# An encoder trunk in two-part fp32: seven half-width products in place of eight for 16 of the 22 up-projection tiles of each feed-forward block

## The chip, the cores and the metric

One Trainium2 chip, one core. The metric is device time in microseconds (us) of one execution. The kernel before takes 2198.45 us, the median of three runs (2198.32 to 2200.83). Smaller is better.

## The reference

Two layers over 512 tokens of 1024 channels. Each layer is a feed-forward block (FFN), a token mixer, a cross-attention into 256 memory tokens and a second FFN, all with a norm ahead and a sum behind. The change is in the FFNs, of which there are four; one step of it is in the cross-attention.

```python
def swiglu(h, w1, w3, w2):            # w1, w3: 1024 x 2816, w2: 2816 x 1024
    return (jax.nn.silu(h @ w1) * (h @ w3)) @ w2

for l in range(DEPTH):                # 2
    x = x + 0.5 * swiglu(rmsnorm(x, ffn1_norm[l]), ffn1_w1[l], ffn1_w3[l], ffn1_w2[l])
    ...                               # mixer
    x = x + mem_cross_attention(rmsnorm(x, xa_norm[l]), rmsnorm(mem, mem_norm[l]),
                                xa_wq[l], xa_wkv[l], xa_wo[l])
    x = x + 0.5 * swiglu(rmsnorm(x, ffn2_norm[l]), ffn2_w1[l], ffn2_w3[l], ffn2_w2[l])
return rmsnorm(x, final_norm)
```

## The kernel before

**Layout.** x lies in SBUF with its channels on the partitions, as eight tiles of 128 channels x 512 tokens (`xall`, also called xT). Every product is made in fp32 with operands in two parts: `split` (L64 to L76) rounds a tile to the width of the PE on ScalarE (`hi`, L72 or L75) and subtracts it from its source on VectorE (`lo`, L73 or L76); `mm3` (L78 to L82) makes hi·hi, hi·lo and lo·hi, three matmuls. So each weight and each activation costs one ACT and one DVE instruction for its split, and three matmuls for each 128 x 128 block of a weight.

**The stream of weights.** `Weights` (L85 to L140) holds all chunks of 128 x 1024 numbers in the order of their use. `load` fetches a chunk (512 KB) by a DMA on the queue of SyncE (SP), seven chunks ahead of its use (HL + RAW); `cut` splits it two ahead. `next` is called once for each chunk by whoever uses it.

**An FFN** (L375 to L410). The 22 column tiles of w1 and w3 are worked in two parts of 11. For a tile, `col_matmul` makes 8 x 3 matmuls of 512 columns (tokens) with a chunk of w1, then as many with a chunk of w3. The gain of the norm is in the split of x (`Norm.part`), its 1/rms is applied behind the products: DVE multiplies the PSUM tile by `rrow` (L390 and L401), ACT takes the silu (L391), POOL (GpSimd) multiplies the two (L402), and the product `ahl` is split for the down projection. `project` (L337) then adds a part's share of the down projection to x (L356, DVE, eight instructions a part), and behind the last part each finished tile of x goes at once into the next norm: `h` on ACT and DVE, its square on ACT (L309), the sum of the squares on POOL (L314).

**The start of the cross-attention** (from L632). The memory lies in SBUF for the whole program, already scaled by its own 1/rms (`memT`). `xattn` splits it with the layer's gain into `mn` (L75 and L76, sixteen instructions), and its first products are `kT`, of 256 columns, from `mn` and the chunks of xa_wk.

**The end.** `finish` turns x over (transposes on PE, L743) while the last part of the down projection is made with tokens on the partitions.

The order of each engine's instructions is fixed when the program is built; an engine takes its instructions in that order. DMAs are issued in order by the engine whose queue they are on.

Of the kernel before, what the change touches and what calls it, by code (L numbers as in the profile page):

```python
# [14 lines left out]
P = 128  # L15
D = 1024
T = 512
# [10 lines left out]
XSCALE = 256.0 ** -0.5  # L28

# Columns of the table of per-channel vectors: name -> columns per layer.  # L30
# [11 lines left out]
def trunk_kernel(ctx: ExitStack, tc: tile.TileContext, ap: dict, out: bass.AP):  # L42
# [4 lines left out]
    wp = ctx.enter_context(tc.tile_pool(name="wp", bufs=3))  # L47
    hp = ctx.enter_context(tc.tile_pool(name="hp", bufs=16))
    sp = ctx.enter_context(tc.tile_pool(name="sp", bufs=19))
# [11 lines left out]
    def h_tile():  # L61
        return hp.tile([P, 512], F32R, tag="h", name="h")
# [15 lines left out]
    def mm3(o, a, b, start, stop):  # L78
        """o += a.T @ b, both in two parts."""
        pe.matmul(o, a[0], b[0], start=start, stop=False)  # L80
        pe.matmul(o, a[0], b[1], start=False, stop=False)  # L81
        pe.matmul(o, a[1], b[0], start=False, stop=stop)  # L82

    # ------------------------------------------------------------------ the stream of weights
    class Weights:  # L85
        """All weight chunks [128, a, b] with a * b <= 1024 in the order of their use: loaded some
        chunks ahead, split two ahead."""
        RAW, HL = 4, 3

        def __init__(self):  # L90
            self.src, self.raw, self.hl, self.at = [], {}, {}, 0

        def cols(self, w, c):
            """Columns c*128.. of a weight of 1024 rows, which lie as [128, 8, 128]."""
            self.src.append((w[c], NK, P))

        def rows(self, w, k, n, lo, hi):
            """Columns lo..hi of the row blocks k..k+n."""
# [6 lines left out]

        def load(self, i):
            if i < len(self.src) and i not in self.raw:
                src, a, b = self.src[i]
                t = wp.tile([P, 1024], F32, tag="raw", name="raw", bufs=self.RAW)
                tv = t[:, :a * b].rearrange("p (a b) -> p a b", b=b)  # L110
                for c in range(0, a, a if i else a // 2):
                    ce = c + (a if i else a // 2)
                    nc.sync.dma_start(tv[:, c:ce], src[:, c:ce])
                self.raw[i] = t

        def cut(self, i):
            if i < len(self.src) and i not in self.hl:
                self.load(i)
                _, a, b = self.src[i]
                if i == len(self.src) - 1:  # L120
                    hi, lo = s_tile([P, 1024], F32R, "whi"), s_tile([P, 1024], F32R, "wlo")
                else:
                    hi = wp.tile([P, 1024], F32R, tag="whi", name="whi", bufs=self.HL)
                    lo = wp.tile([P, 1024], F32R, tag="wlo", name="wlo", bufs=self.HL)
                n = a * b
                step = n if i else n // 2
                for c in range(0, n, step):
                    split(hi[:, c:c + step], lo[:, c:c + step], self.raw[i][:, c:c + step])
                self.hl[i] = tuple(t[:, :n].rearrange("p (a b) -> p a b", b=b) for t in (hi, lo))

        def next(self):
            i = self.at
            self.at += 1
            for j in range(i, i + self.HL):
                self.cut(j)
            if i + self.HL == len(self.src) - 1:
                self.cut(i + self.HL)
            for j in range(i, i + self.HL + self.RAW):
# [10 lines left out]
    for l in range(L):  # L149
        for w1, w3, w2 in (("ffn1_w1", "ffn1_w3", "ffn1_w2"), ("ffn2_w1", "ffn2_w3", "ffn2_w2")):  # L150
            for half in range(2):
                n = NJ // 2
                for j in range(half * n, (half + 1) * n):
                    wts.cols(ap[w1][l], j)
                    wts.cols(ap[w3][l], j)
                if half and w1 == "ffn2_w1" and l == L - 1:
                    for k in [*range(n)] * 2:
                        wts.rows(ap[w2][l], n + k, 1, 0, D)
                else:
                    wts.project(ap[w2][l][half * n * P:(half + 1) * n * P, :], n)  # L160
# [16 lines left out]
    # ------------------------------------------------------------------ x, channels on partitions  # L177
# [29 lines left out]
    # ------------------------------------------------------------------ lower bounds and memory  # L207
# [3 lines left out]
    def lower_bounds():  # L211
        """Softmax over the layers, summed up to each, less the first."""
# [18 lines left out]
    memT = const.tile([P, NK, M], F32, name="memT")  # L231
# [651 lines left out]
```

## Time and profile before

| | |
|---|---|
| median of the runs | 2198.45 us |
| the profiled execution, first to last instruction (span) | 2195.1 us |
| PE busy | 2171.9 us, 99% |
| DVE busy | 1164.9 us, 53% |
| ACT busy | 721.2 us, 33% |
| POOL busy | 316.4 us, 14% |
| mean granted clock of PE | 0.998 |

The profiled execution is known by its span; the median of the runs is 3.35 us above it. A busy PE is one with matmuls in its pipe: two matmuls that follow one another overlap in the rows, so what a matmul costs is the distance from its start to the next one's, not its duration. "Idle before, releaser" at the end of a row says how long the engine had waited and what ended it.

### The profile page before, as it was taken

What the parts mean: (1) busy time and instruction counts of PE and PEld (TensorE: products, weight loads), DVE (VectorE), ACT (ScalarE), POOL (GpSimd) and SP (SyncE); (2) the same over time, 40 slices, a digit from 0 to 9 for tenths busy, and PEclk for the clock granted to TensorE, in tenths of its full rate; (3) what the DMA queues carried; (4) which work ended last, traced back from release to release, by engine and by line L of the source; (5) the groups of instructions that cost most, each with busy time, mean ns of one, the idle gap of its engine ahead of it and who ended that gap; (6) DMA issues with size and microseconds to landing.
All of it is one profiled execution on the core that took longest, in us unless ns stands there. A gap on an engine that the chain in (4) does not pass through costs nothing.

```text
span 2195.1 us, 25372 instructions
## 1 busy us (share of the span) xinstructions
PE 2171.9 (99%) x10166; PEld 1812.4 (83%) x10166; DVE 1164.9 (53%) x1668; ACT 721.2 (33%) x991; POOL 316.4 (14%) x249
## 2 busy tenths in 40 slices
PE   8999999999999999999999999999999999999998
PEld 6888888788988888888888888887889888888886
DVE  6534544777635544345355345357775455543545
ACT  5322223313434422222332223233144443222234
POOL 3100111302200210011021001023121002100102
PEclk9999999999999999999999999999999999999999
DMA  5323332221432333332333233232214323323334
GB/s 207 96 91 101 96 103 94 87 68 49 132 99 88 95 96 96 96 102 87 100 101 99 88 104 98 96 101 77 68 54 129 97 88 96 96 94 99 98 119 156
DMA packets 75253, 216.40 MB, mean 99 GB/s; under 512 B 6912, under 2 KB 6912, under 8 KB 75008
## 3 DMA queue, kind: packets, MB, share of 16 engines
q1 hardware_dynamic: 74272, 213.16, 30.9%
q8 instruction: 80, 1.31, 0.2%
q10 hardware_dynamic: 864, 1.63, 0.2%
q14 instruction: 37, 0.30, 0.0%
HBM read 212.66 MB, written 2.10 MB: 98 GB/s over the span
## 4 chain that ended last, share of the span: by engine, by line
PE 97%; DVE 2%; POOL 1%; ACT 0%; issue 0%; DMA 0%; SPq 0%; POOLq 0%; DVEq 0%; ACTq 0%
PE ps L80 23%; PE ps L81 23%; PE ps L82 23%; PE acc L81 7%; PE acc L80 7%; PE acc L82 7%; PE ps L495 2%; PE ps L617 0%; DVE wlo L73 0%; POOL qk L448 0%; PE ps L618 0%; PE ps L601 0%; PE ps L522 0%; PE ps L259 0%; PE acc L259 0%
## 5 line engine op out<-in xcount | busy, mean ns | idle before, releaser
L73 DVE TENSOR_TENSOR wlo<-raw,whi 128x1024 fp32r<-128x1024 f32 (+1 forms) x403 | 584.2, 1450 | 423.6 <-ACT whi L72 423.6
L72 ACT CAST whi<-raw 128x1024 fp32r<-128x1024 f32 (+1 forms) x403 | 416.8, 1035 | 1183.8 <-PE ps L81 609.9
L80 PE MATMUL ps<-h,whi 128*128 128x512 f32 x1848 | 720.7, 391 | 7.7 <-ACT h L75 7.7
L81 PE MATMUL ps<-h,whi 128*128 128x512 f32 x1848 | 720.9, 390 | 0.6 <-DVE h L76 0.6
L82 PE MATMUL ps<-h,wlo 128*128 128x512 f32 x1848 | 720.3, 390 | 0.0
L80 PEld LDWEIGHTS ps<-h,whi 128*128 128x128 f32 x1848 | 348.1, 188 | 80.7 <-ACT h L75 8.1
L81 PEld LDWEIGHTS ps<-h,whi 128*128 128x128 f32 x1848 | 347.9, 188 | 73.5 <-DVE h L76 1.8
L82 PEld LDWEIGHTS ps<-h,wlo 128*128 128x128 f32 x1848 | 347.8, 188 | 72.5 <-DVE wlo L73 0.2
L402 POOL TENSOR_TENSOR t<-t,t 128x512 f32<-128x512 f32 x88 | 122.2, 1389 | 1022.9 <-ACT whi L72 915.2
L401 DVE TENSOR_TENSOR t<-ps,rrow 128x512 f32<-128x512 f32 x87 | 60.1, 691 | 261.9 <-PE ps L82 261.9
L390 DVE TENSOR_TENSOR t<-ps,rrow 128x512 f32<-128x512 f32 x88 | 60.8, 691 | 127.6 <-PE ps L82 120.9
L80 PE MATMUL ps<-ahl,whi 128*128 128x512 f32 x308 | 119.8, 389 | 0.0
L81 PE MATMUL ps<-ahl,whi 128*128 128x512 f32 x308 | 119.8, 389 | 0.0
L80 PE MATMUL acc<-ahl,whi 128*128 128x512 f32 x308 | 119.8, 389 | 0.0
L81 PE MATMUL acc<-ahl,whi 128*128 128x512 f32 x308 | 119.8, 389 | 0.0
L82 PE MATMUL acc<-ahl,wlo 128*128 128x512 f32 x308 | 119.8, 389 | 0.0
L82 PE MATMUL ps<-ahl,wlo 128*128 128x512 f32 x308 | 118.7, 389 | 0.0
L314 POOL TENSOR_TENSOR sqa<-sqa,sq 128x512 f32<-128x512 f32 x48 | 76.2, 1587 | 140.7 <-ACT sq L309 138.7
L72 ACT CAST ahl<-t 128x512 fp32r<-128x512 f32 x88 | 54.9, 624 | 117.2 <-POOL t L402 117.2
L76 DVE SCALAR_TENSOR_TENSOR h<-xall,vec,h 128x512 fp32r<-128x512 f32 x64 | 73.5, 1171 | 24.3 <-ACT h L75 24.0
L81 PE MATMUL acc<-h,whi 128*128 128x512 f32 x200 | 78.1, 390 | 0.0
L82 PE MATMUL acc<-h,wlo 128*128 128x512 f32 x200 | 78.0, 390 | 0.0
(205 smaller groups left out, 2311.9 us busy)
## 6 DMA issues: line engine op xcount, KB each, us to landing
raw<-in_ffn_w_dram SPq DMA_DIRECT2D x267, 512.0 KB, 3.6
raw<-in_w_in_dram SPq DMA_DIRECT2D x32, 512.0 KB, 3.5
raw<-in_w_out_dram SPq DMA_DIRECT2D x16, 512.0 KB, 3.6
raw<-in_xa_wk_dram SPq DMA_DIRECT2D x16, 512.0 KB, 3.5
raw<-in_xa_wq_dram SPq DMA_DIRECT2D x16, 512.0 KB, 3.5
raw<-in_xa_wv_dram SPq DMA_DIRECT2D x16, 512.0 KB, 3.6
raw<-in_xa_wo_dram SPq DMA_DIRECT2D x16, 512.0 KB, 3.7
raw<-in_ffn_w_dram SPq DMA_DIRECT2D x16, 256.0 KB, 2.6
```

Of the source, the lines that this page charges most:

```text
L72: act.copy(hi, src)
L73: dve.tensor_tensor(lo, src, hi.bitcast(F32), op=ALU.subtract)
L76: dve.scalar_tensor_tensor(lo, src, scale, hi.bitcast(F32), op0=ALU.mult, op1=ALU.subtract)
L80: pe.matmul(o, a[0], b[0], start=start, stop=False)
L81: pe.matmul(o, a[0], b[1], start=False, stop=False)
L82: pe.matmul(o, a[1], b[0], start=False, stop=stop)
L314: pool.tensor_tensor(a, self.sq, s, op=ALU.add)
L390: dve.tensor_tensor(t1, p1, norm.r, op=ALU.mult)
L401: dve.tensor_tensor(t3, p3, norm.r, op=ALU.mult)
L402: pool.tensor_tensor(t3, t1, t3, op=ALU.mult)
L495: pe.matmul(o, kg[g][:, hh, sl], rhs, start=True, stop=True)
```

## The change

**Pairs of tiles.** In each FFN the first 6 of the 22 tiles stay as they were (PLAIN). The other 16 are worked as 8 pairs, and each pair once with w1 and once with w3: 16 blocks in an FFN, 64 in the program. A block is the product of two column tiles of a weight (2 x 128 columns, 1024 rows, seen as 2 x 2 blocks) with the activations (1024 rows in two halves, 512 tokens in two halves of 256). It is made from 7 half products instead of 8 (Strassen's scheme in Winograd's form): 7 x 4 x 3 = 84 matmuls of 256 columns where two `col_matmul` made 48 of 512.

**The right operands** (`Pairs.operands`, L472 to L533): x times gain times 1/rms by DVE (8 instructions of 512), four sums of its quarters by DVE (L493 and L496, 2 instructions of 512 each), and seven splits of 1024 columns (b11, b21, b22, t1 to t4). They are made between the products of tiles 2 to 5 of the same FFN. 1/rms is now in the operands, so the products need no scaling behind them.

**The left operands** (`Weights.load`, `cut`). For a block the SP queue brings two halves of 256 KB (L130, L131) into a tile `wsum`, the first tile (L132, 512 KB) and the lower half of the second (L133, 256 KB). Then a DMA on the queue of GpSimd *adds* the whole second tile (512 KB) to what lies in `wsum` (L134): this makes two of the four sums of left blocks in SBUF. It waits for both halves. DVE makes the other two sums (L163, L164; 512 columns each). Split are r1, s1, s2 (1024 columns each) and w22 (512).

**Behind the products** of a block: three copies of 256 PSUM columns by ACT (`keep`, L537), four sums of a PSUM tile and a kept one in halves of 256 columns by DVE (L592, L610 and, with the product by the gate in the same instruction, L618), the silu on ACT. The gate product is made by DVE (L612, L614, L618); POOL has none in a block. The last two of the seven products of a block are made among the first of the next one (`open`).

**Other steps.** The down projection runs in three parts (8, 8 and 6 tiles) instead of two of 11, so x is added to three times in an FFN. One pool of 38 slots of 4 KB takes the place of three pools. `memT` is no longer kept: each layer loads it again (four DMAs on the SP queue), and DVE multiplies it by its 1/rms (L914, four instructions of 512) right ahead of the splits into `mn`.

```diff
+PLAIN = 6
+PARTS = ((0, 8), (8, 16), (16, 22))
 ...
         def load(self, i):
+            if len(self.src[i]) == 2:
+                c1, c2 = self.src[i]
+                s1, t1 = s_tile([P, NK, P], F32, "wsum"), s_tile([P, NK, P], F32, "raw")
+                t2 = s_tile([P, 4, P], F32, "raw")
+                nc.sync.dma_start(s1[:, :4], c1[:, :4])
+                nc.sync.dma_start(s1[:, 4:], c2[:, :4])
+                nc.sync.dma_start(t1, c1)
+                nc.sync.dma_start(t2, c2[:, 4:])
+                nc.gpsimd.dma_start(s1, c2, accum_op=ALU.add)
...
         def cut(self, i):
+                split(h0, l0, r1)
+                split(h1, l1, s1)
+                dve.tensor_tensor(s2[:, :512], s1[:, 512:], a11, op=ALU.add)
+                dve.tensor_tensor(s2[:, 512:], s2[:, :512], a12, op=ALU.add)
+                split(h2, l2, s2)
+                split(t[:, 0], t[:, 1], a22)
...
+        def block(self, out):
+            w = wts.next()
+            last, self.open = self.open, None
+            z, y, x = ps_tile(), acc_tile(), acc_tile()
+            self.product(z, "a11", "b11", True)
+            c1 = self.keep(z)
+            if last:
+                last[0]()
+            self.product(y, "s1", "t1", True)
+            p5 = self.keep(y)
+            self.product(x, "a12", "b21", True)
+            out.add(0, 0, x, c1)
+            if last:
+                last[1]()
+            self.product(z, "q", "t2", False)
+            u = self.keep(z)
+            self.product(y, "f", "b22", False)
+            out.add(0, 1, y, u)
...
     def xattn(l, norm, after):
         for k2 in range(NK // 2):
+            mt = s_tile([P, 2, M], F32, "mt")
+            nc.sync.dma_start(mt, ap["memT"][:, 2 * k2:2 * k2 + 2])
+            dve.tensor_tensor(mt, mt, memr.rearrange("p (o m) -> p o m", o=1).broadcast_to([P, 2, M]), op=ALU.mult)
             t = s_tile([P, 2, 2, M], F32R, "mn")
             for e in range(2):
                 k = 2 * k2 + e
-                split(t[:, 0, e], t[:, 1, e], memT[:, k], scale=vcol("mem_norm", l, k))
+                split(t[:, 0, e], t[:, 1, e], mt[:, e], scale=vcol("mem_norm", l, k))
```

**Three places of the order.** The first is VectorE in the first FFN. Before, around two tiles (`t1`, `t3` are the scaled PSUM tiles):

```order
L390 TENSOR_TENSOR t_782<-ps,rrow 128x512
L73 TENSOR_TENSOR wlo<-raw,whi 128x1024
L401 TENSOR_TENSOR t_816<-ps,rrow 128x512
L73 TENSOR_TENSOR wlo<-raw,whi 128x1024
L73 TENSOR_TENSOR ahl<-t_816,ahl 128x512
```

In the changed program, one gate block and the first half of the up block behind it, in the steady part (`wsum`: sums of left blocks; `raw`: tiles as loaded):

```order
L77 TENSOR_TENSOR wlo_1779<-raw_1494,whi_1778 128x1024
L592 TENSOR_TENSOR gate_1751<-acc_1763,keep_1776 128x256
L77 TENSOR_TENSOR wlo_1811<-wsum_1493,whi_1810 128x1024
L163 TENSOR_TENSOR wsum_1827<-wsum_1493,raw_1494 128x512
L618 SCALAR_TENSOR_TENSOR up_1621<-ps_1630,gate_1492 128x256
L164 TENSOR_TENSOR wsum_1827<-wsum_1827,raw_1494 128x512
L77 TENSOR_TENSOR ahl_1490<-up_1621,ahl_1490 128x512
L592 TENSOR_TENSOR gate_1751<-acc_1762,keep_1857 128x256
L77 TENSOR_TENSOR wlo_1860<-wsum_1827,whi_1859 128x1024
L77 TENSOR_TENSOR w22_1877<-raw_1495,w22_1877 128x512
L77 TENSOR_TENSOR wlo_1902<-raw_1623,whi_1901 128x1024
L592 TENSOR_TENSOR gate_1752<-ps_1761,keep_1808 128x256
```

For a pair of tiles VectorE had 10 instructions (twice the five above); it now has 23, from `wlo_1779` to the L612 of the next up block: 6 wlo, 2 w22, 4 sums of weights, 2 ahl, 6 sums of 256 columns, L612 and L618 of 256 columns, and L614 of 512.

The second place is VectorE at the start of the first layer's cross-attention. Before (the last additions to x are the two L356):

```order
L76 SCALAR_TENSOR_TENSOR mn<-memT,vec,mn 128x256 x8
L73 TENSOR_TENSOR wlo<-raw,whi 128x1024
...
L356 SCALAR_TENSOR_TENSOR xall<-acc,xall 128x512 x2
L76 SCALAR_TENSOR_TENSOR h<-xall,vec,h 128x512
L356 SCALAR_TENSOR_TENSOR xall<-acc,xall 128x512 x2
L76 SCALAR_TENSOR_TENSOR h<-xall,vec,h 128x512
L73 TENSOR_TENSOR wlo<-raw,whi 128x1024
L76 SCALAR_TENSOR_TENSOR h<-xall,vec,h 128x512 x2
L73 TENSOR_TENSOR wlo<-raw,whi 128x1024
L73 TENSOR_TENSOR kT<-ps,kT 128x256
```

In the changed program:

```order
L430 SCALAR_TENSOR_TENSOR xall<-acc,xall 128x512
L80 SCALAR_TENSOR_TENSOR h<-xall,vec,h 128x512 x2
L914 TENSOR_TENSOR mt<-mt,memr 128x512
L80 SCALAR_TENSOR_TENSOR mn<-mt,vec,mn 128x256 x2
L335 TENSOR_SCALAR v<-acc 128x4
L914 TENSOR_TENSOR mt<-mt,memr 128x512
L938 TENSOR_SCALAR sr<-rcol 128x4
L80 SCALAR_TENSOR_TENSOR mn<-mt,vec,mn 128x256 x2
L914 TENSOR_TENSOR mt<-mt,memr 128x512
L80 SCALAR_TENSOR_TENSOR mn<-mt,vec,mn 128x256 x2
L914 TENSOR_TENSOR mt<-mt,memr 128x512
L80 SCALAR_TENSOR_TENSOR mn<-mt,vec,mn 128x256 x2
```

The splits of the memory, which stood ahead of the last additions to x, now stand behind the last `h`, each pair of them behind its own L914.

The third place is TensorE at the same point of the changed program (before, the first `ps<-mn` follows the last `acc<-h` directly):

```order
L86 MATMUL acc_5046<-h_4976,wlo_5090 128x512
L333 MATMUL acc_5458<-ones_88,sqa_5223 128x1 x4
L84 MATMUL ps_5257<-mn_5228,whi_5133 128x256
L84 MATMUL ps_5291<-mn_5228,whi_5163 128x256
L85 MATMUL ps_5257<-mn_5228,whi_5133 128x256
L86 MATMUL ps_5257<-mn_5228,wlo_5134 128x256
L84 MATMUL ps_5257<-mn_5228,whi_5133 128x256
```

The products that lead to 1/rms of the next norm (L333, from the sum of squares `sqa`, which POOL makes) have moved ahead of the first products with `mn`; before they came behind six of the eight tiles of `kT`. The first two tiles of `kT` (`ps_5257`, `ps_5291`) are now worked side by side, one pair of `mn` after the other.

## Rows read from the trace of the kernel before

**Rows 1.** The page: the span, the busy time of the engines, and the chain that ended last, by engine.

```profile
span 2195.1 us, 25372 instructions
PE 2171.9 (99%) x10166; PEld 1812.4 (83%) x10166; DVE 1164.9 (53%) x1668; ACT 721.2 (33%) x991; POOL 316.4 (14%) x249
PE 97%; DVE 2%; POOL 1%; ACT 0%; issue 0%; DMA 0%; SPq 0%; POOLq 0%; DVEq 0%; ACTq 0%
```

**Rows 2.** The two largest of the three waits of TensorE in the whole span: us in total, times, longest.

```profile
PE ps L80 <- ACT h L75: 7.7, 1, 7.7
PE ps L455 <- DVE atd L482: 6.6, 2, 3.3
```

**Rows 3.** The timeline of TensorE (start and duration in us) in a stretch of products of 512 columns: the first and the last of 49 rows without idle time between them, 48 distances.

```profile
410.18 0.39 PE L80 MATMUL ps<-h,whi 128*128 128x512 f32 x1
...
421.06 0.39 PE L80 MATMUL ps<-h,whi 128*128 128x512 f32 x1
```

**Rows 4.** The timeline of TensorE at the start of the first layer's cross-attention: the last product of 512 columns, the first of 256, and the one 48 distances behind that.

```profile
577.22 0.39 PE L82 MATMUL acc<-h,wlo 128*128 128x512 f32 x1
577.44 0.28 PE L80 MATMUL ps<-mn,whi 128*128 128x256 f32 x1
...
583.20 0.28 PE L80 MATMUL ps<-mn,whi 128*128 128x256 f32 x1
```

**Rows 5.** Groups of instructions on VectorE by form over the whole span: count, then busy us and mean ns of one, then the idle time before them and its releasers.

```profile
L73 DVE TENSOR_TENSOR wlo<-raw,whi 128x1024 fp32r<-128x1024 f32 x387 | 573.1, 1482 | 370.6 <-ACT whi L72 370.6
L73 DVE TENSOR_TENSOR ahl<-t,ahl 128x512 fp32r<-128x512 f32 x88 | 61.2, 697 | 13.1 <-ACT ahl L72 12.8
L390 DVE TENSOR_TENSOR t<-ps,rrow 128x512 f32<-128x512 f32 x88 | 60.8, 691 | 127.6 <-PE ps L82 120.9 <-ACT rrow L326 6.7
L73 DVE TENSOR_TENSOR kT<-ps,kT 128x256 fp32r<-128x256 f32 x16 | 6.7, 416 | 0.0
L76 DVE SCALAR_TENSOR_TENSOR mn<-memT,vec,mn 128x256 fp32r<-128x256 f32 x16 | 6.5, 484 | 0.0
```

**Rows 6.** The timeline of VectorE around two of its splits of weights in the second part of the first FFN.

```profile
303.76 2.33 DVE L73 TENSOR_TENSOR wlo<-raw,whi 128x1024 fp32r<-128x1024 f32 x1 [0.21 <-ACT whi L72]
...
309.20 1.23 DVE L73 TENSOR_TENSOR wlo<-raw,whi 128x1024 fp32r<-128x1024 f32 x1 [0.21 <-ACT whi L72]
```

**Rows 7.** The timeline of POOL in the same stretch: the only instruction there.

```profile
303.72 1.29 POOL L402 TENSOR_TENSOR t<-t,t 128x512 f32<-128x512 f32 x1 [8.46 <-ACT whi L72]
```

**Rows 8.** Groups on ScalarE by form, columns as in rows 5.

```profile
L72 ACT CAST whi<-raw 128x1024 fp32r<-128x1024 f32 x387 | 406.9, 1052 | 1121.0 <-PE ps L81 579.2 <-issue 281.7 <-PE acc L81 155.7
L391 ACT ACTIVATE t<-t 128x512 f32<-128x512 f32 x88 | 55.1, 626 | 1.0 <-DVE t L390 1.0
L72 ACT CAST kT<-ps 128x256 fp32r<-128x256 f32 x16 | 5.9, 366 | 0.0
L75 ACT ACTIVATE mn<-memT,vec 128x256 fp32r<-128x256 f32 x16 | 6.6, 496 | 0.0
```

**Rows 9.** The page's DMA parts: a queue (packets, MB, share of the span of 16 engines), and issues (count, KB each, median us from issue to landing).

```profile
q1 hardware_dynamic: 74272, 213.16, 30.9%
raw<-in_ffn_w_dram SPq DMA_DIRECT2D x267, 512.0 KB, 3.6
raw<-in_ffn_w_dram SPq DMA_DIRECT2D x16, 256.0 KB, 2.6
```

**Rows 10.** The timeline of VectorE from the splits of the memory to the first products of the first layer's cross-attention.

```profile
545.33 3.26 DVE L76 SCALAR_TENSOR_TENSOR mn<-memT,vec,mn 128x256 fp32r<-128x256 f32 x8
...
577.64 0.69 DVE L356 SCALAR_TENSOR_TENSOR xall<-acc,xall 128x512 f32<-128x512 f32 x1 [0.61 <-PE acc L82]
578.25 1.28 DVE L76 SCALAR_TENSOR_TENSOR h<-xall,vec,h 128x512 fp32r<-128x512 f32 x1
579.45 1.21 DVE L73 TENSOR_TENSOR wlo<-raw,whi 128x1024 fp32r<-128x1024 f32 x1
580.59 3.49 DVE L76 SCALAR_TENSOR_TENSOR h<-xall,vec,h 128x512 fp32r<-128x512 f32 x2
```

**Rows 11.** The timeline of POOL in the same stretch: the last two sums of squares of the norm.

```profile
579.80 3.73 POOL L314 TENSOR_TENSOR sqa<-sqa,sq 128x512 f32<-128x512 f32 x2 [0.81 <-ACT sq L309]
```

**Rows 12.** The timeline of TensorE in the first part of the program: two matmuls of 512 columns that follow one another, and the first two at a closer distance.

```profile
12.28 0.63 PE L81 MATMUL ps<-h,whi 128*128 128x512 f32 x1
12.70 0.63 PE L82 MATMUL ps<-h,wlo 128*128 128x512 f32 x1
...
16.11 0.44 PE L80 MATMUL ps<-h,whi 128*128 128x512 f32 x1
16.39 0.39 PE L81 MATMUL ps<-h,whi 128*128 128x512 f32 x1
```

**Rows 13.** The timeline of TensorE behind one of its two waits in the mixer (the time in brackets is the idle time before the row).

```profile
434.13 0.71 PE L455 MATMUL ps<-qkp,ones_r 128*128 128x512 f32 x2 [3.28 <-DVE atd L482]
...
434.98 0.39 PE L81 MATMUL ps<-h,whi 128*128 128x512 f32 x1
435.20 0.39 PE L82 MATMUL ps<-h,wlo 128*128 128x512 f32 x1
```

**Rows 14.** The timeline of TensorE in `finish`: twelve turned blocks, that is three half rows of tokens.

```profile
2123.30 1.47 PE L743 MATMUL ps<-fixed,xall 128*128 128x128 f32 x12
```

**Rows 15.** The timeline of ScalarE there: the copies of those three.

```profile
2126.21 1.55 ACT L744 COPY y<-ps 128x512 f32<-128x512 f32 x3
```

More of the change, by code (lines that the diff above doesn't have):

```diff
@@ L104, in project @@
                     self.rows(w, g[0], len(g), half * 512, (half + 1) * 512)
-        def load(self, i):
[L107 to L114, printed above, removed]
@@ L116, in cut, with ahead @@
-        def cut(self, i):
[L117 to L121, printed above, removed]
-                else:
[L123 to L129, printed above, removed]
+        def ahead(self, i, n):
+            m = 0
+            while i < len(self.src) and m < n:
+                yield i
+                m += 2 if len(self.src[i]) == 2 else 1
+                i += 1
@@ L131, in next, with step, first @@
+        def step(self):
+            while self.todo:
+                if next(self.todo[0], self) is self:
+                    self.todo.pop(0)
+                else:
+                    return
+        def first(self):
+            self.todo.append(self.cut(0))
+            self.step()
         def next(self):
@@ L133, in next @@
             self.at += 1
[L134 to L138, printed above, removed]
+            while self.todo:
+                self.step()
+            block = len(self.src[i]) == 2
+            ahead = [*self.ahead(i, self.SPLIT + block)]
+            if i + self.SPLIT == len(self.src) - 1:
+                ahead.append(i + self.SPLIT)
+            for j in ahead:
+                if j not in self.hl:
+                    self.todo.append(self.cut(j))
+                    if not block or j == i:
+                        while self.todo:
+                            self.step()
+            for j in self.ahead(i, self.LOAD):
                 self.load(j)
@@ L249, in prepare_mem @@
         pr = col_to_row(dg, 2)
-        for k2 in range(NK // 2):
-            t = memT[:, 2 * k2:2 * k2 + 2]
-            dve.tensor_tensor(t, t, pr[:, :M].rearrange("p (o m) -> p o m", o=1).broadcast_to([P, 2, M]), op=ALU.mult)
+        act.copy(memr, pr[:, :M])
     def col_rsqrt(sq, inv, tag, tile=acc_tile):
@@ new lines, in trunk_kernel, with __init__, add, done @@
+    class Gate:
+        def __init__(self):
+            self.t = [tp.tile([P, T], F32, tag="gate", name="gate", bufs=4) for _ in range(2)]
+        def add(self, i, half, ps, t):
+            o = self.t[i][:, half * HT:(half + 1) * HT]
+            dve.tensor_tensor(o, ps[:, :HT], t, op=ALU.add)
+            if half:
+                o = self.t[0] if i == 0 else o
+                act.activation(o, o, AF.Silu, scale=-1.0 if i else 1.0)
+        def done(self, ps):
+            act.activation(self.t[1][:, :HT], ps[:, :HT], AF.Silu, scale=-1.0)
@@ L374, in ffn @@
     def ffn(norm, after, start=None, between=None):
-        n = NJ // 2
-        for half in range(2):
+        pairs = None
+        for lo, hi in PARTS:
             a = []
-            for jj in range(n):
-                if start and half == 0 and jj < 2:
-                    if jj == 0:
+            for j in range(lo, hi):
+                if j >= PLAIN:
+                    ahl = s_tile([P, 2, T], F32R, "ahl")
+                    a.append((ahl[:, 0], ahl[:, 1]))
+                    if j % 2:
+                        gate = Gate()
+                        pairs.block(gate)
+                        pairs.block(Up(gate, a[-2:]))
+                        if between:
+                            next(between, None)
+                    continue
+                if start and j < 2:
+                    if j == 0:
@@ L392, in ffn @@
                 norm.then(left)
+                if j == 2:
+                    pairs = Pairs(norm)
+                    operands = pairs.operands()
+                if j > 1:
+                    next(operands, None)
+                    next(operands, None)
                 if p3 is None:
@@ L407, in ffn @@
                     next(between, None)
-            if half and after is None:
+                if j > 1:
+                    next(operands, None)
+                    next(operands, None)
+            for _ in operands:
+                pass
+            pairs.close()
+            if hi == NJ and after is None:
                 return a
-            project(n, a, 0.5, after if half else (lambda d: None))
+            project(hi - lo, a, 0.5, after if hi == NJ else (lambda d: None), tiles=(acc_tile, ps_tile))
     def mix(l, norm, after):
@@ L789, in trunk_kernel @@
     norm = Norm("ffn1_norm", 0, late=3)
-    wts.cut(0)
+    wts.first()
     for d in range(NK):
```

231 lines of the change are left out of this document (192 added, 39 removed).

## The prediction

> **What bounds the kernel now.** I read the page first. TensorE is busy 99% of the span and is 97% of the chain that ended last [rows 1]. Then its waits: one of 7.7 us at the start of the program, two of 3.3 us in the mixer, nothing worth naming in an FFN [rows 2]. So the kernel is bound by the number of matmuls times the distance between them, and every other engine is spare. The change removes work from TensorE and gives work to VectorE. It pays as far as TensorE goes on without waiting.
>
> **What TensorE saves.** 48 matmuls of 512 columns take 421.06 − 410.18 = 10.88 us, 0.2267 each [rows 3]. 48 of 256 columns take 583.20 − 577.44 = 5.76 us, 0.120 each, a little more than half [rows 4]. A block has 84 of the latter, 10.08 us, where two tiles with one weight took 10.88. It saves 0.80 us, and 64 blocks save **51.2 us**. Seven eighths of 10.88 would be 9.52; the other 0.56 goes to the narrower matmul's extra time.
>
> A rule speaks for more. The Trainium skill (TensorE: Matmul & The Clock Gate, Wait — 56ns, not 53.3ns?) gives the distance of warm matmuls as columns over 2.4 GHz plus some 2.5 ns: 0.109 us for 256 columns and 0.216 for 512, by which the saving would be 64 × (10.36 − 9.17) = 76 us, an estimate from that page. The trace has 0.120 and 0.2267 instead; I take the rows.
>
> **What the blocks ask of the others.** VectorE runs 23 instructions for a pair of tiles, in the 20.16 us of two blocks. Priced by form [rows 5]: 2 w22, 4 sums and L614 at 0.69 are 4.8 us; 2 ahl at 0.68 are 1.4; 6 sums of 256 columns from PSUM at 0.42 and two products at 0.48 are 3.5. The 6 wlo I take at 1.23, not at their mean of 1.48. The mean holds those that run beside a product of POOL, 2.33 us against 1.23 [rows 6, 7], and in the blocks POOL makes no product. That is 7.4. The sum is 17.0 of 20.16 us, 84%: full, but under. ScalarE has 6 casts of 1024 at 1.05, seven of 256 and 512 columns, and the silus, some 12.3 us by its forms [rows 8]; no bound. A wait of VectorE for a transfer or for ScalarE delays what stands behind it (the sums that free PSUM tiles, the splits of the next block). The weights are split about one block ahead, so waits of 2 or 3 us are covered. I put nothing for the steady blocks.
>
> **The transfers.** For a block 1.25 MB come by SP's queue, and the DMA that adds brings 0.5 MB more. In all 16 engines 213.16 MB took 30.9% of the span, 678 us, so 512 KB take 1.67 us of all engines [rows 9]; 1.25 MB take 4.2 of the block's 10.08. No row shows a DMA that adds. From below it costs what a plain one does, 3.6 us from issue to landing, behind the two halves' 2.6 [rows 9]. From above I set no bound but the turning point: it becomes the bound of the blocks when it takes over 5.9 us of all engines, 3.5 times a plain one, or 10.08 us by itself, if one must end before the next begins. SP issues a block's halves about two blocks of work ahead of their split (loads run seven chunks ahead, splits four, and a block counts as two; with the slots that come free in time some 20 us), so 2.6 + 10 us would still be in time. I take no cost; cover: those 20 us. On POOL L134 waits for the two halves; behind it stand the last gate products of the plain tiles (1.39 us each before, and their ahl is used only in the down projection, blocks later) and otherwise the next L134, so this wait has nobody behind it who is in a hurry. On SP the halves wait for free slots as the loads did before.
>
> The Trainium skill (DMA: Bandwidth & Descriptors, Anatomy of one DMA) has a fit for plain transfers issued by GpSimd, 2.0 us plus the bytes over 436 GB/s: 3.2 us for 512 KB, an estimate; by that the sum stays as it is.
>
> **The start of the cross-attention**, twice. Before, the splits of the memory were done 29 us ahead of their use [rows 10], and the product with `mn` followed the last one of the mixer without a gap [rows 4]. Now L914 and the splits stand behind the last `h`. From the last product's end (577.44) on: the last addition ends at 578.33; three h of 0.75 (undisturbed) bring it to 580.6, and as they ran (1.28 and 3.49 beside POOL's sums of squares [rows 10, 11]), without the wlo between them, to 582.9. Then L914 0.69, ScalarE's mn 0.50 twice, the second mn of VectorE 0.48 [rows 5, 8]: 2.17 us a pair, and the next L914 waits behind it. The first of the four pairs is there 4.4 to 7.6 us after 577.44; L333 waits for `sqa`, at most until 583.5 [rows 11], which is no later. The last pair comes 6.5 us behind the first; meanwhile TensorE has 3 × 12 matmuls of 256, 4.3 us. The loss is 6.6 to 9.8 us. I take 8.5, nearer to the disturbed rows, because POOL's sums still run there: **17 us** for two layers. Half clock could come on top: in the program's first part matmuls of 512 columns followed at 0.43 us, 1.2 GHz, until 16.11 and at 0.28 from there on [rows 12]; behind 3.28 us of idle time they follow at 0.22, 2.4 GHz [rows 13]. No row shows 5 to 8 us of idle time inside the program. The slow rows from 12.28 to 16.11 lose 1.9 us against full clock, and the slow stretch began before them; so I put 0 to 4 us each, take 0 and keep 8 for the range. The skill's rule on that page (What's actually happening), that an idle array falls back to the slow clock, speaks for the upper end.
>
> **The start of the pairs**, four times. The seven operands are made beside tiles 2 to 5: 4 × 10.88 = 43.5 us [rows 3]. VectorE's own part is 8 wlo (9.8), 12 instructions behind products (8.3), 8 scalings (6.0), 8 half sums (5.5) and the splits of the operands (9.1): 38.7 us, or 43.1 when four wlo run beside POOL's products [rows 5, 6]. It is full, and the first block's own 3.5 splits and 2 sums come into the same stretch. What is late is t3 and t4 and the first block's sums, each a chain of sum, cast and subtraction (1.4 + 1.05 + 1.23 = 3.7). Between 0 and two such chains (7.3) an FFN; I take 2, nearer to none since 38.7 is under 43.5: **8 us**, 0 to 29.
>
> **The rest.** `finish` now turns its last five half rows one behind another (before, three at a time among products [rows 14]): each copy takes 0.52 us [rows 15], their PSUM tiles come free so late, and the first split waits behind them: **3 us**, 0 to 5. Eight more additions to x in an FFN, 0.69 each, lie beside the products of a third pass of the down projection, where VectorE is idle; if that cover went, 5.5 us an FFN. The four DMAs of memT a layer go ahead of their use by the chunks between; nothing.
>
> **Sum.** The profiled span 2195.1 − 51.2 + 17 + 8 + 3 = 2171.9. The median of the runs stands 3.35 above that execution: **2175 us**. By the bounds of the terms: 2195.1 − 51.2 + 13 + 0 + 0 + 3.35 = 2160 to 2195.1 − 51.2 + 20 + 8 + 29 + 5 + 3.35 = 2209.
>
> **Rivals.**
> *VectorE becomes the bound of the blocks (slower).* 84% is counted with every wlo at 1.23. Each wlo that runs as in rows 6 adds 1.10 to the 17.0 of a pair. The block phases have 32 pairs; the 23 us that are left of the gain are gone when a pair takes 0.7 us more than 20.16, so at 20.9, which four stretched wlo of the six reach (21.4): 2175 + 32 × 1.24 = 2215 us. For it: the share is counted, not seen, GpSimd still works for its DMA, and waits come on top of a busy share. Against: in the blocks POOL has no product of its own. 0.13.
> *The DMA that adds becomes the bound (slower).* At 12 us each, one after another, 64 × 1.9 = 123 us: 2298; break-even at 10.4 us. For it: no row has its price. Against: that is 2.9 times a plain transfer. 0.07.
> *Nearly all of the gain stays.* The scheduler's order hides the starts better than counted; the xattn loss at 6.6 and nothing else: 2160 or, if the memory's splits do not wait for the last h, 2150. For it: 38.7 is under 43.5. Against: the order of VectorE at the cross-attention is fixed. 0.12.
> *The starts cost all of the gain (no change).* Starts at 5 an FFN or more, and the half clock: 2195 to 2206. 0.10.
>
> **How the numbers follow.** The forecast has 0.58 (2163 to 2190). About 0.2% of the time, 4.4 us, is what a measurement can tell from no change. Faster: forecast, nearly all, and a little of the last case: 0.58 + 0.12 + 0.02 = 0.72. Same: 0.05 of the last case and 0.02 of VectorE's: 0.07. Slower: 0.21. The range leaves out 0.05 below and about 0.15 above (most of the two slower rivals): 2154 to 2209.
>
> **What would show it.** Right: distances of 0.120 in the blocks, no wait of TensorE inside a run of blocks, a gap of 5 to 8 us ahead of the first product with `mn` ended by VectorE's mn, smaller ones at the first blocks of each FFN ended by splits or sums, VectorE near 84% in a stretch of blocks with wlo near 1.23. Wrong: TensorE waiting in every block, for wlo behind a `wsum` (the transfers) or for wlo with VectorE busy throughout (VectorE's bound); or distances other than 0.120.

## The result and the profile after

The changed kernel takes 2180.98 us (median; 2179.93 to 2181.34), against 2198.39 us of the kernel before on the same chip: a ratio of 0.9918, with a 95% interval from 0.9907 to 0.993. It is faster by 17.4 us; the forecast was 23.

The page of the changed kernel, the lines that answer to [rows 1, 9]:

```profile
span 2179.3 us, 31306 instructions
PE 2135.4 (98%) x12470; PEld 1886.3 (87%) x12470; DVE 1403.0 (64%) x2212; ACT 886.7 (41%) x1372; POOL 289.8 (13%) x249
q1 hardware_dynamic: 93520, 228.37, 31.6%
q0 software_dynamic: 9216, 33.56, 9.0%
PE 90%; DVE 5%; ACT 2%; issue 1%; POOL 1%; DMA 0%; SPq 0%; POOLq 0%; ACTq 0%; DVEq 0%
wsum<-in_ffn_w_dram POOLq DMA_DIRECT2D x64, 512.0 KB, 5.6
```

TensorE's busy time fell by 36.5 us only, and its idle time rose from 23.2 to 43.9 us (span less busy time). Its waits (us in total, times, longest), against [rows 2]:

```profile
PE acc L333 <- POOL sqa L388: 9.8, 2, 4.9
PE ps L84 <- ACT h L79: 7.4, 1, 7.4
PE acc L84 <- ACT whi L76: 5.6, 6, 1.7
PE ps L86 <- DVE wlo L77: 3.9, 7, 1.0
PE ps L725 <- DVE atd L752: 2.6, 2, 1.3
```

A block in the steady part, on TensorE's timeline: two rows 84 distances apart, 10.08 us, 0.120 each. Between them stands no idle time:

```profile
885.11 0.28 PE L84 MATMUL ps<-bh,whi 128*128 128x256 f32 x1
...
895.19 0.28 PE L86 MATMUL ps<-bh,wlo 128*128 128x256 f32 x1
```

Where the time went, by stage. A stage runs from the first matmul of one kind to that of the next on TensorE's timeline:

| stage | before, us | after, us | difference |
|---|---|---|---|
| first FFN, from the program's start | 373.38 | 372.81 | −0.6 |
| mixer, layer 1 | 204.06 | 208.95 | +4.9 |
| cross-attention, layer 1 (to its last projection) | 110.35 | 114.17 | +3.8 |
| that projection and the second FFN | 409.56 | 396.87 | −12.7 |
| third FFN | 360.49 | 349.72 | −10.8 |
| mixer, layer 2 | 205.35 | 208.92 | +3.6 |
| cross-attention, layer 2 | 110.36 | 114.20 | +3.8 |
| projection, fourth FFN, `finish` | 421.55 | 413.66 | −7.9 |

The border between a cross-attention and the projection behind it holds a shift: eight of its products of 512 columns (1.8 us), which came behind the first product of the projection, now come ahead of it. So 1.8 us of each +3.8 belong to the stage below. 16 blocks of an FFN should save 12.8 us. With the shift taken out the second FFN gives 10.9, the third 10.8, the fourth 6.1 and the first nearly nothing, and the stages from mixer to cross-attention cost 12.5. The first FFN and these passages are where the experiments look.

### The profile page after: what moved, and what is told of

It is laid out like the page before. It is cut to its first block, busy times and chain, and to the rows that moved or that the text cites. A ratio compares the mean times of both kernels' runs of the same rounds, so it can differ in the third digit from the quotient of the medians.

```text
span 2179.3 us, 31306 instructions
## 1 busy us (share of the span) xinstructions
PE 2135.4 (98%) x12470; PEld 1886.3 (87%) x12470; DVE 1403.0 (64%) x2212; ACT 886.7 (41%) x1372; POOL 289.8 (13%) x249
## 3 DMA queue, kind: packets, MB, share of 16 engines
q1 hardware_dynamic: 93520, 228.37, 31.6%
## 4 chain that ended last, share of the span: by engine, by line
PE 90%; DVE 5%; ACT 2%; issue 1%; POOL 1%; DMA 0%; SPq 0%; POOLq 0%; ACTq 0%; DVEq 0%
PE ps L86 17%; PE ps L84 17%; PE ps L85 17%; PE acc L84 11%; PE acc L85 11%; PE acc L86 11%; PE ps L765 2%; DVE wlo L77 1%; ACT whi L76 1%; DVE h L80 1%; PE ps L885 0%; POOL t L666 0%; DVE bsum L496 0%; DVE qkp L77 0%; PE ps L886 0%
## 5 line engine op out<-in xcount | busy, mean ns | idle before, releaser
L84 PE MATMUL ps<-h,whi 128*128 128x512 f32 x824 | 322.9, 393 | 8.8 <-ACT h L79 7.4
L85 PE MATMUL ps<-h,whi 128*128 128x512 f32 x824 | 321.5, 391 | 2.2 <-DVE h L80 2.2
L86 PE MATMUL ps<-h,wlo 128*128 128x512 f32 x824 | 321.0, 391 | 2.6 <-DVE wlo L77 2.6
L84 PE MATMUL acc<-bh,whi 128*128 128x256 f32 x768 | 218.2, 285 | 4.5 <-ACT whi L76 3.8
L84 PE MATMUL ps<-bh,whi 128*128 128x256 f32 x768 | 217.6, 284 | 1.2 <-ACT whi L76 1.2
L86 PE MATMUL ps<-bh,wlo 128*128 128x256 f32 x768 | 217.7, 284 | 0.5 <-DVE wlo L77 0.5
L85 PE MATMUL ps<-bl,whi 128*128 128x256 f32 x768 | 217.5, 283 | 0.0
L85 PE MATMUL acc<-bl,whi 128*128 128x256 f32 x768 | 217.4, 283 | 0.0
L86 PE MATMUL acc<-bh,wlo 128*128 128x256 f32 x768 | 217.1, 284 | 0.0
L84 PEld LDWEIGHTS ps<-h,whi 128*128 128x128 f32 x824 | 155.2, 188 | 41.8 <-ACT h L79 7.4
L85 PEld LDWEIGHTS ps<-h,whi 128*128 128x128 f32 x824 | 155.2, 188 | 36.8 <-DVE h L80 5.4
L86 PEld LDWEIGHTS ps<-h,wlo 128*128 128x128 f32 x824 | 155.1, 188 | 36.7 <-DVE wlo L77 4.3
L134 POOL DMA_DIRECT2D wsum<-in_ffn_w_dram x64 | 55.6, 869 | 777.8 <-PE ps L86 260.2
```

Of the source, the lines that this page charges most:

```text
L84: pe.matmul(o, a[0], b[0], start=start, stop=False, skip_group_check=more)
L85: pe.matmul(o, a[0], b[1], start=False, stop=False, skip_group_check=more)
L86: pe.matmul(o, a[1], b[0], start=False, stop=stop, skip_group_check=more)
L134: nc.gpsimd.dma_start(s1, c2, accum_op=ALU.add)
```

## The experiments

All are variants of the changed kernel (2181.0 us). The kernel before ran beside each at 2198.5 to 2199.0 us.

**e1: the memory's part ahead of the mixer's last projection.** Its loads, L914 (L690 in this file) and the splits go into a function `memory(l)`:

```diff
+        self_mn.append(memory(l))
         project(NK, parts, 1.0, after, order=MIX_OUT, tiles=(acc_tile, acc_tile),
...
     def xattn(l, norm, after):
-        mn = []
-        for k2 in range(NK // 2):
...
+        mn = self_mn.pop()
```

> Only the place of the memory's part is changed: its loads, L914 and the splits into mn are written ahead of the mixer's last projection instead of behind it. The changed kernel has 4.9 us of waiting for sqa and then products with mn at the pace of VectorE at both cross-attentions, 8.3 us lost each. Theory (the late mn costs it): about 14 to 17 us faster than the changed kernel, 2164 to 2168 us, and no idle time between the last product of the mixer and the first with mn. Rival (the work of VectorE is only moved: the outputs of the mixer's heads come later by as much): under 6 us faster, 2175 or more, with new waits of TensorE in the mixer's last part.

2180.42 us, ratio 0.9919 (0.9904 to 0.9934): no gain; the rival held. The products with `mn` now follow without a wait, but TensorE's timeline has a new one at the projection, and 1.2 GHz behind it (0.42 and 0.43 us between matmuls of 512 columns):

```profile
547.60 0.80 PE L84 MATMUL acc<-h,whi 128*128 128x512 f32 x1 [5.70 <-ACT whi L76]
```

ScalarE shows why: that split stands behind the four pairs of `mn`, which wait for L914 one after another:

```profile
538.57 0.91 ACT L79 ACTIVATE mn<-mt,vec 128x256 fp32r<-128x256 f32 x2 [3.04 <-DVE mt L690]
...
545.70 0.91 ACT L79 ACTIVATE mn<-mt,vec 128x256 fp32r<-128x256 f32 x2 [1.22 <-DVE mt L690]
546.51 1.03 ACT L76 CAST whi<-raw 128x1024 fp32r<-128x1024 f32 x1
```

**e2: the second weight chunk split behind the fourth h.**

```diff
     for d in range(NK):
         norm.part(d)
+        if d == 3:
+            wts.todo.append(wts.cut(1))
+            wts.step()
```

> Only the place of one split is changed: that of the second weight chunk stands behind the fourth h instead of behind the eighth, as in the kernel before. Theory (the first FFN loses 6.5 us at the program's start, because TensorE needs this chunk before the last h): 4 to 7 us faster than the changed kernel, 2174 to 2177 us, and the waits for h and wlo before 21 us gone or shorter. Rival (the eight loads that the larger pool lets through at once slow the transfers of x): no gain, within 2 us of 2181.

2174.61 us, ratio 0.9891 (0.9876 to 0.9905), 6.4 us faster than the changed kernel: the theory's number held. In the changed kernel VectorE made the last four h and then five splits of weights in a row:

```profile
12.19 6.29 DVE L80 SCALAR_TENSOR_TENSOR h<-xall,vec,h 128x512 fp32r<-128x512 f32 x4 [0.49 <-ACT h L79]
18.40 7.95 DVE L77 TENSOR_TENSOR wlo<-raw,whi 128x1024 fp32r<-128x1024 f32 x5
```

so TensorE, which had only the first chunk's products until then, waited for three of the h and then for the split (the last two of the four waits):

```profile
18.53 0.50 PE L85 MATMUL ps<-h,whi 128*128 128x512 f32 x1 [0.73 <-DVE h L80]
20.77 0.50 PE L86 MATMUL ps<-h,wlo 128*128 128x512 f32 x1 [1.04 <-DVE wlo L77]
```

Before, that split ran ahead of the last h:

```profile
13.05 2.31 DVE L73 TENSOR_TENSOR wlo<-raw,whi 128x1024 fp32r<-128x1024 f32 x1
```

In e2 none of these waits (three for h, one for wlo) is left. The eight loads that pass at once are the same in e2 as in the changed kernel, so they were not the cause. What in the building of the program moved the split was not looked for.

But the 6.4 us are not what the changed kernel had lost here against the kernel before. The 48th product of 512 columns with `h`, in the kernel before, the changed kernel and e2:

```profile
23.22 0.39 PE L80 MATMUL ps<-h,whi 128*128 128x512 f32 x1
25.66 0.39 PE L86 MATMUL ps<-h,wlo 128*128 128x512 f32 x1
20.76 0.39 PE L86 MATMUL ps<-h,wlo 128*128 128x512 f32 x1
```

The changed kernel is 2.4 us late at this point, and e2 is 2.5 us ahead of the kernel before. The lead of e2 over the changed kernel then stays between 4 and 5.4 us up to `finish`. There the granted clock of the changed kernel falls to 1.2 GHz for 3.4 us (from 2142.6 on), in e2's profile it does not, and this gives e2 another 1.3 us.

**e3: VectorE makes all four sums.**

```diff
-                nc.sync.dma_start(s1[:, :4], c1[:, :4])
-                nc.sync.dma_start(s1[:, 4:], c2[:, :4])
                 nc.sync.dma_start(t1, c1)
-                nc.sync.dma_start(t2, c2[:, 4:])
-                nc.gpsimd.dma_start(s1, c2, accum_op=ALU.add)
+                nc.sync.dma_start(t2, c2)
...
+                dve.tensor_tensor(s1[:, :512], a11, c2[:, :512], op=ALU.add)
+                dve.tensor_tensor(s1[:, 512:], c2[:, :512], a22, op=ALU.add)
                 split(h1, l1, s1)
```

> The DMA that adds is left out: SP loads both tiles of a block whole, and VectorE makes the two sums too, two more instructions of 512 columns a block, 2.8 us a pair. VectorE was busy 51.2 of 70 us in a steady stretch, 14.7 of 20.16 us a pair. Theory (VectorE has room in the blocks, and the DMA that adds costs and saves nothing there): 17.5 of 20.16, no wait of TensorE in steady blocks, 2181 to 2186 us (1 us more at each start of pairs). Rival (VectorE is near its bound, and the DMA that adds is what keeps it below): over 2195 us, with waits in the steady blocks.

2196.57 us, ratio 0.9989 (0.998 to 0.9999): 15.6 us slower, over the theory's range, and yet not in the way of the rival. The waits of TensorE:

```profile
PE ps L86 <- DVE wlo L77: 11.2, 16, 3.1
PE acc L334 <- POOL sqa L389: 9.8, 2, 4.9
```

None of them lies in the steady blocks, which go on at 0.120 us. Apart from those for sqa most lie at the starts of the pairs and in the plain tiles just ahead of them, and in two FFNs 1.2 GHz follows there. An FFN loses 4 to 5 us against the changed kernel in the profiled execution. So the DMA that adds is worth 15.6 us here, where VectorE is nearly full by the count of the prediction, and nothing in the blocks. Whether VectorE's load costs it there, or the longer chain of sums ahead of a split, is not told apart.

**e4: one product of seven left out.**

```diff
             def third():
-                self.product(z, "c1", "t3", False)
                 out.add(1, 1, z, p5)
```

> One of the seven products of each block (c1 with t3) is left out, 12 matmuls of 256 columns in each of 64 blocks, so part of the up-projection is missing. All else stays. Theory (the blocks are bound by TensorE alone): 64 x 12 x 0.120 = 92 us faster than the changed kernel, 2089 us, give or take 4; VectorE would then be busy 14.7 of 17.3 us. Rival (the other engines are near their bound): at least 15 us of this are not given, over 2104 us.

2090.5 us, ratio 0.951 (0.9494 to 0.9526): 90.5 us faster, of 92.2 worked out. The blocks are bound by TensorE, with room for the others in 17.3 us a pair.

**e5: e2, and the memory's part ahead of the outputs of the mixer's heads, with L914 on POOL (L691 there), all four ahead of the splits.**

```diff
+        self_mn.append(memory(l))
         pooled(3), pooled(2), read(0), pooled(1), read(1), scale(0), pooled(0), read(2), scale(1), emit(0)
...
-            dve.tensor_tensor(mt, mt, memr.rearrange("p (o m) -> p o m", o=1).broadcast_to([P, 2, M]), op=ALU.mult)
+            pool.tensor_tensor(mt, mt, memr.rearrange("p (o m) -> p o m", o=1).broadcast_to([P, 2, M]), op=ALU.mult)
```

> Beside the early split of e2, the memory's part is written ahead of the outputs of the mixer's heads, and its four multiplications by 1/rms (L914) are made by POOL, all four before the splits. In e1 TensorE waited 5.7 us for the first split of the projection, because the chain of four times L914 on VectorE, mn on ScalarE, mn on VectorE (9 us) stood on both engines just ahead of it. Theory (what costs is this chain in a place where TensorE needs the two engines; taken apart and put where they are idle it costs nothing): 12 to 17 us faster than e2, 2158 to 2163 us, no wait for sqa, no wait of 5.7 us in the mixer. Rival (any place in the mixer only moves the loss, since its last part is bound by VectorE and ScalarE): within 4 us of e2's 2174.6.

2163.28 us, ratio 0.9839 (0.9825 to 0.9854): 11.3 us faster than e2, just short of the theory's 12 to 17, and 1.6% faster than the kernel before. The wait for sqa is gone, and so is the half clock behind it; a wait of 1.7 us a layer has come (VectorE's qf in the mixer, where POOL now multiplies):

```profile
PE ps L811 <- DVE qf L821: 3.4, 2, 1.7
```

No other kernel run here is as fast, but for e4, which leaves a product out. It beats both kernels.

**e6: memT kept, as in the kernel before.** `memT` in SBUF, scaled once in the first FFN, L914 left out, `SLOTS = 36` for its 8 KB; no other edit.

> Of the changed kernel only the memory is put back: memT is kept in SBUF, scaled once, as in the kernel before (for its 8 KB the pool has 36 slots instead of 38). L914 is gone from the cross-attention; the order still has the eight splits into mn behind the last h. Theory (the chain costs, and its place): the wait for sqa of 4.9 us stays; the pace behind it gains, some 2 us a layer: 2174 to 2179 us. Rival (L914 itself is the whole loss): 14 us or more faster than the changed kernel, 2167 or less.

2193.87 us, ratio 0.9978 (0.9968 to 0.9987): 13 us slower than the changed kernel, and both theories missed. At the passage to the cross-attention it wins nothing: from the first product of the mixer to the first product that has `mn` as its moving operand, 284.45 us against 284.12. Without L914 the splits of `mn` still stand behind the last h, and TensorE waits for them in place of sqa:

```profile
576.72 0.51 PE L84 MATMUL ps<-mn,whi 128*128 128x256 f32 x2 [2.19 <-ACT mn L79]
579.73 0.58 PE L85 MATMUL ps<-mn,whi 128*128 128x256 f32 x1 [2.50 <-DVE mn L80]
```

So L914 itself is not the loss. The 13 us come elsewhere: 4 us of waits at each start of pairs, where the changed kernel has 1.2 in three FFNs.

**e8: the changed kernel with `SLOTS = 36`.**

> The changed kernel with a pool of 36 slots in place of 38, nothing else. e6, which kept memT and so had 36 slots, was 13 us slower than the changed kernel, with 4 us of waits at each start of pairs where the changed kernel has 1.2. Theory (two slots fewer do that: the splits and operands at the start of the pairs wait for slots): 8 to 16 us slower than the changed kernel, 2189 to 2197 us, with waits of TensorE for whi and wlo around each start of pairs as in e6. Rival (something else in e6, the larger constant or the missing loads of memT): within 4 us of 2181.

2193.86 us, ratio 0.9976 (0.9965 to 0.9986): the same time as e6. One start of pairs on TensorE's timeline (third FFN), where the changed kernel has 0.23 and 0.95 us:

```profile
1159.13 0.50 PE L84 MATMUL ps<-h,whi 128*128 128x512 f32 x1 [0.91 <-ACT whi L76]
1160.39 0.50 PE L86 MATMUL ps<-h,wlo 128*128 128x512 f32 x1 [0.53 <-DVE wlo L77]
1171.14 0.39 PE L84 MATMUL ps<-bh,whi 128*128 128x256 f32 x1 [1.16 <-ACT whi L76]
1172.40 0.39 PE L86 MATMUL ps<-bh,wlo 128*128 128x256 f32 x1 [0.48 <-DVE wlo L77]
```

Two slots of 38 are worth 13 us: the 8 KB that letting go of memT made free.

**e7: the right operands begun one step earlier (with e2's edit).**

```diff
-                if j == 2:
-                    pairs = Pairs(norm)
-                    operands = pairs.operands()
...
                 a.append((ahl[:, 0], ahl[:, 1]))
...
+                if j == 1:
+                    pairs = Pairs(norm)
+                    operands = pairs.operands()
```

> Beside the early split of e2, the seven right operands are begun behind tile 1 instead of tile 2, so that VectorE has half a tile more for them. Theory (at the start of the pairs VectorE is late by the work that does not fit beside tiles 2 to 5: waits of 2.7 us and some half clock in the first FFN, 1.2 us in the others): 2 to 6 us faster than e2, 2169 to 2172.5. Rival (what is late there are the first block's own sums and casts, a chain that depends on the transfers and its order, not on VectorE's load): within 1.5 us of e2's 2174.6.

2177.99 us, ratio 0.9903 (0.9887 to 0.992): 3.4 us slower than e2; the theory fell, and the rival's number (within 1.5 us) too. In the first FFN the waits have moved into the plain tiles (1.18, 0.68, 1.41 and 1.54 us for whi and wlo), with half clock behind them; in the three others the wait of 0.96 us at the first blocks became one of 0.88 in the last plain tile. The work that VectorE has to do there is the same. Some 1.3 us of the difference is again the half clock in `finish`, which this profile has and e2's has not.

**e9: e5's POOL version at e1's place.**

> As e5 (early split of the second chunk, L914 on POOL, all four ahead of the splits), but written where e1 had it, right ahead of the mixer's last projection. It tells the chain from the place. Theory (in that place the chain of L914 and mn, 9 us long, was the loss; eight splits in a batch take 3.3 us, as in the kernel before): 2162 to 2166 us, like e5, with a wait of at most 2 us ahead of the projection. Rival (the place is the loss: ScalarE and VectorE are needed there for the first split of the projection): 2169 to 2175 us, with a wait of 4 us or more for whi.

2172.65 us, ratio 0.9879 (0.9864 to 0.9895), only 2 us faster than e2: the rival held, with a wait of 3.9 us where it had said 4 or more.

```profile
540.99 0.80 PE L84 MATMUL acc<-h,whi 128*128 128x512 f32 x1 [3.89 <-ACT whi L76]
```

e5 and e9 differ in the place alone, and it is worth 9.4 us. With e1 and e6 this says that the loss is the place more than L914 or its engine: e6 has no L914 and gains nothing at the passage, and e9, with L914 on POOL and ahead of all splits, gains 2 us where e1 gained none. Behind the last h or ahead of the projection the splits stand where TensorE's next operand comes from the same two engines; ahead of the heads' outputs they don't. e5's place with L914 on VectorE was not run.

## Why the prediction was right

The mechanism was right: TensorE is the bound, the blocks give what their distances say, and the losses lie where something other than the steady work begins. The time lay 6 us above the forecast, within the range. That it came so near owes something to luck, since terms that were wrong partly cancelled. What a matmul costs is its distance to the next, so the terms below are distances beyond 0.227 us (512 columns) and 0.120 (256); a wait costs some 0.16 us more than its idle time, because the row of the matmul ahead of it lasts that much longer than its distance (0.28 against 0.12).

**The saving, 51.2 us.** Right: 0.120 us in the blocks as in [rows 4], 84 a block, and e4 gave back 90.5 of the 92.2 us that a product's share is worth.

**VectorE in the blocks, 17.0 of 20.16 us.** Right that it is no bound, the size too high. In two pairs of the steady part, with busy us (and rows) of each engine, then PEclk, the DMA share and GB/s:

```profile
885.00:925.32 40.32, 40.32 (x339) 40.32 (x338) 29.58 (x47) 21.40 (x37) 2.58 (x3) 1.00 0.58 149
```

VectorE is busy 14.8 us a pair, 73%. The wlo are undisturbed as assumed, but rows of instructions that follow directly overlap, so that the sum of durations counts some 0.09 us of each twice:

```profile
820.40 0.42 DVE L592 TENSOR_TENSOR gate<-ps,keep 128x256 f32<-128x256 f32 x1
820.74 1.22 DVE L77 TENSOR_TENSOR wlo<-wsum,whi 128x1024 fp32r<-128x1024 f32 x1
821.87 0.69 DVE L163 TENSOR_TENSOR wsum<-wsum,raw 128x512 f32<-128x512 f32 x1
```

The first of the rivals, with 0.13, was further off than its 20.9 us suggested.

**The DMA that adds, no cost.** Right. It lands 5.6 us after its issue; q0's 9.0% of 2179.3 us, over 64, is 3.1 us of all 16 engines for 512 KB, against 1.6 of a plain one (31.6% of 2179.3 us for 228.37 MB). That is 1.9 times, where 3.5 was the turning point. By the fit in the Trainium skill (DMA: Bandwidth & Descriptors, Anatomy of one DMA), which is for plain transfers, it would have been 3.2 us to landing, an estimate; the trace has 5.6 and decides.

**The start of the cross-attention, 17 us.** Right: 17.6. From the last product of the mixer on, the same 153 matmuls (the eight L333 and the first 144 with `mn` among them) end their places at 595.53 in the kernel before, 18.3 us after 577.22 [rows 4], and at 601.88 in the changed one, 27.1 us after 574.75; the second layer has 18.3 and 27.1 too:

```profile
595.53 0.36 PE L80 MATMUL ps<-mn,whi 128*128 128x256 f32 x1
601.88 0.28 PE L84 MATMUL ps<-mn,whi 128*128 128x256 f32 x1
```

The stages lost only 12.5 us, because the mixers gained 5.1 that the sum did not have: 2 us less waiting for atd in each (1.3 us against 3.3 [rows 2]), and in the second the half clock that had followed this wait. The course was as worked out, but the lower bound of the first pair, 4.4 us, counted only up to ScalarE's first `mn`; by its own rows (3.2 + 2.17) it is 5.3. The wait is put down to L333, which stands first in TensorE's order, but the first pair of `mn` came no earlier: the last product of the mixer ends its place at 574.97, VectorE's two `mn` are done at 582.0, 7.1 us later, within what was given. h and L914 ran disturbed by POOL's sums. TensorE, then VectorE:

```profile
574.75 0.39 PE L86 MATMUL acc<-h,wlo 128*128 128x512 f32 x1
580.03 1.87 PE L333 MATMUL acc<-ones,sqa 128*128 128x1 f32 x8 [4.89 <-POOL sqa L388]
...
582.33 0.41 PE L85 MATMUL ps<-mn,whi 128*128 128x256 f32 x1
582.54 0.41 PE L86 MATMUL ps<-mn,wlo 128*128 128x256 f32 x1
...
586.28 0.28 PE L86 MATMUL ps<-mn,wlo 128*128 128x256 f32 x1
586.40 0.28 PE L85 MATMUL ps<-mn,whi 128*128 128x256 f32 x1
```

```profile
576.03 2.82 DVE L80 SCALAR_TENSOR_TENSOR h<-xall,vec,h 128x512 fp32r<-128x512 f32 x2
578.78 1.75 DVE L914 TENSOR_TENSOR mt<-mt,memr 128x512 f32<-128x512 f32 x1
581.16 0.88 DVE L80 SCALAR_TENSOR_TENSOR mn<-mt,vec,mn 128x256 fp32r<-128x256 f32 x2 [0.64 <-ACT mn L79]
582.03 0.68 DVE L914 TENSOR_TENSOR mt<-mt,memr 128x512 f32<-128x512 f32 x1
583.70 0.87 DVE L80 SCALAR_TENSOR_TENSOR mn<-mt,vec,mn 128x256 fp32r<-128x256 f32 x2
```

The pairs came 2.1 to 2.5 us apart, as worked out (2.17). And the half clock, which I kept for the range, is there: 0.21 us between matmuls of 256 columns, 1.2 GHz, up to 586, and 0.12 from there on. I had taken 0 for it. What it costs cannot be told from these rows, since TensorE waits for `mn` between them too. The rule that I had cited for it (the Trainium skill, TensorE: Matmul & The Clock Gate, What's actually happening), that an idle array falls back to the slow clock, agrees with these rows. My row for the other side was one of two: behind the wait of [rows 13] the clock stayed, but behind the same wait in the second layer of the kernel before it fell (rows at the end).

**The start of the pairs, 8 us.** Somewhat low: 10.5, within its 0 to 29. In each of three FFNs 1.2 us of waits cost 1.7; in the first 2.7 us of waits and 15 matmuls at 0.21 cost 5.4. **`finish`, 3 us:** 0.5 and 1.8 us of waits and six distances of 0.43, 4.7 in all, near the top of its 0 to 5.

**What failed.** The sum had no term for the first FFN ahead of its pairs, and 6.6 us were lost there. The last product of the plain tiles, the 288th with `h`, before and after:

```profile
79.39 0.39 PE L82 MATMUL ps<-h,wlo 128*128 128x512 f32 x1
86.02 0.39 PE L86 MATMUL ps<-h,wlo 128*128 128x512 f32 x1
```

2.4 us of it are there by the 48th product (e2). I had looked at the three places of the order where the diff has an edit; the second chunk's split had moved too, at the program's start, and e2 shows that the waits there hang on it. By the 144th product the loss is 4.2 us, with a wait of 1.4 us for the first scaled `t` (L648); the rest comes with waits of 0.50, 0.84 and 0.22 us for wlo in tiles 2 to 5, where the operands are made. These stand in e2 as well, and their cause was not looked for. The sum had put the whole cost of the operands at the first blocks.

With the terms as measured: 2195.1 − 51.2 + 12.5 + 10.5 + 4.7 + 6.6 = 2178.2 us against the span of 2179.3; 1.1 us are left. Against the forecast's 2171.9 the passages came out 4.5 lower, by the mixers' gain, and the other three 10.8 higher. The median lay 1.7 us above the profiled execution, where I had added 3.35.

## What to carry to other kernels

Where one engine is the bound, the saving is the number of its instructions times the distance between them, and it came out to within 2 us of 92 (e4); the losses lay at passages, where something other than the steady work begins. So read the order of every passage, also of those where the diff has no edit: one split that had moved gave some 5 us when it was put back, and two slots of 38 were worth 13 us. A gain over the changed kernel is not yet the size of its loss against the kernel before: compare the same instruction in all three. A chain that goes to and fro between two engines is to be put where the bound engine doesn't need either of them; making it shorter in the wrong place gained 2 us, the other place 11.

## What the runs showed of the hardware

In the kernel before, TensorE went on at 2.4 GHz behind one wait of 3.28 us [rows 13], and at 1.2 GHz for 3 us behind the other, in the second layer (0.43 us between matmuls of 512 columns):

```profile
1518.59 1.19 PE L455 MATMUL ps<-qkp,ones_r 128*128 128x512 f32 x2 [3.28 <-DVE atd L482]
1519.58 0.63 PE L80 MATMUL ps<-h,whi 128*128 128x512 f32 x1
1520.01 0.63 PE L81 MATMUL ps<-h,whi 128*128 128x512 f32 x1
```

Behind 3.9 (e9), 4.9 (the changed kernel) and 5.7 us (e1) it went on at 1.2 GHz for 3 to 6 us. In the first FFN of the changed kernel it fell to 1.2 GHz (0.21 us between matmuls of 256 columns from 94.7 to 97.7 us) behind three waits of 0.44, 1.21 and 0.49 us only; in e5 and e9 the same three waits (0.44, 1.22 and 0.48 or 0.49 us) left it at 2.4 GHz. So the same waits are followed by either clock, and a time holds a few us of half clock that another run of the same instructions can lack.

In e9 an instruction of VectorE on 128x4 numbers took 1.20 us beside a product of POOL, and 0.15 without:

```profile
531.88 1.20 DVE L346 TENSOR_TENSOR clo<-ocol,chi 128x4 f32<-128x4 f32 x1
...
539.26 0.15 DVE L346 TENSOR_TENSOR clo<-ocol,chi 128x4 f32<-128x4 f32 x1
```
